# Attention to SSD passage: the time-step chain on 128 partitions, its projections around tile 1's norm, norms by columns, later transposes

## The chip, the cores and the metric

The kernel runs on one core of a Trainium2 chip. The metric is the device time of one execution in microseconds (us). The engines are PE (matmuls), PEld (weight loads), DVE (vector), ACT (scalar functions and copies), POOL (GpSimd) and SP, which issues most of the DMAs. A difference of under 0.3% is not told apart from none here.

## The reference

Two layers over a latent of 1024 tokens and a context of 256, width 1024: gated windowed attention, then a gated bidirectional Mamba-2 SSD mixer. Cut to what the change touches:

```python
# every layer: u = rms_normalize(h) * (1 + scale) + shift; h = h + gate * mixer(u)
def rms_normalize(x):
    return x * lax.rsqrt(jnp.mean(x * x, axis=-1, keepdims=True) + EPS)

def front(h):                       # SSD mixer, for ctx and for the latent
    z, xbc, dt_raw = jnp.split(h @ w_in, [...], axis=-1)
    xbc = jax.nn.silu(centred_depthwise_conv(xbc, conv_w, conv_b))
    xs, bm, cm = jnp.split(xbc, [...], axis=-1)
    dt = jax.nn.softplus(dt_raw.reshape(..., 2, GROUPS, HEADS_PER_GROUP) + dt_bias)
    return z, xs, bm, cm, dt

# scan of one direction, chunks of 128 tokens
da = dt * -exp(a_log)
a_cs = jnp.cumsum(da, axis=2)       # within the chunk
decay_to_end = jnp.exp(a_last - a_cs)
states = einsum(bm, decay_to_end, x * dt)
h_next = exp(a_last) * h_prev + states
y = einsum(cm . bm, exp(a_cs_q - a_cs_s), x * dt) + einsum(cm, h_prev, exp(a_cs))
```

The time steps dt are 64 numbers a token: 32 heads in each of two directions. The backward direction cumulates from the end of a chunk.

## The kernel before

**Tiles.** Tokens are cut into tile 0 and tile 1 (512 latent tokens each) and tile 2 (the 256 context tokens). Activations lie with features on partitions. Every matmul operand is split into a high and a low part (`wh`, `wl` from a raw weight tile `wr`: ACT copy L212 or L952, POOL or DVE difference L214 or L956; `uH`, `uL` of the activations), and a product is three matmuls (L226 to L228, or L1003 and L1012 in the SSD's own loops), each of 256 or 512 columns.

**The end of the attention layer.** `out_steps(i)` yields, for a tile, eight steps `one(m)` and then `fin`. A step loads two halves of an output weight (L219), loads the residual, projects, adds the gated product to the residual on DVE (L723, into `h1k` for tile 1), stores it (L724), squares it on ACT (L727 for m = 0, else L730) and adds the square to the sum `sqa` on POOL (L731). `fin` makes the norm with `rstd`: one matmul with a matrix of ones (L258), a square root on ACT (L260, whose table has to be loaded), a reciprocal on DVE (L261). Then `modulate` runs for each of eight 128-row chunks: DVE multiplication by r (L287), ACT scale and shift (L288), ACT copy to `uH` (L289), DVE difference to `uL` (L290). The steps of tiles 2 and 0 are spread among the attention blocks of tile 1; those of tile 1 come last.

**The other norm.** `rstd_c` and `rstd_n` exist already and serve the first layer's norm. One matmul for each 128 tokens puts the sums on partitions (L342, one column), ACT scales them (L350), POOL raises four numbers a partition to the power -1/2 (L351), DVE spreads them on a diagonal (L353), a matmul with ones broadcasts it (L355), ACT copies the result out (L357).

**The time steps.** `ssd_consts` loads the dt weights (L841, split at L843 and L845), projects tiles 2, 0 and 1 to 64 rows (64 dt numbers on partitions, tokens along the row), evicts with the bias (L862), and runs one chain for the context and tile 0 (64 x 768) and one for tile 1 (64 x 512). A chain is the softplus (L870 to L881, with Exp and Ln on ACT), the logarithm of dt (L882), the two cumulative sums (L886, L887, one for each direction), a store of them to DRAM (L888), the totals and their exponentials (stores L895, L897), differences and exponentials (L900 to L906). Then each 128-token chunk is turned with PE transposes of 64 x 64 (L910, L913, L914, L917 into `psX`; two chunks, the context's, need only the first) and copied out by ACT (L911, L915, L916, L918) and DVE (L919, `vd`). Last, `eal` is read back to all partitions (L920). All ten chunks are turned in `ssd_consts`.

**The SSD's front.** `front(g)` is a generator for one group of heads. It projects, weight column by weight column, bT, two x tiles (x0, x1) and cT, each for the context (`psD`, L1003) and the latent (`pj2`, L1012), followed by the convolution taps and silu as `post` steps, and, for the first three, transposes (L976) that ACT copies out (L979). Then come the gates z (L1037, 256 columns). `post` is a list of steps worked off between matmuls; an entry `(LATE, steps)` waits until so many us of matmuls have gone by. Two groups interleave in slots later: a slot handles a chunk and a direction, with states (L1106, L1164), the POOL product `xw` (L1081), and so on.

**What sets the order.** A scheduler fixes each engine's order when the kernel is built; DMAs of SP run in the order of its queue. In the SSD layer the weight pools `wr`, `wh`, `wl` have two buffers each.

Of the kernel before, what the change touches and what calls it, by code (L numbers as in the profile page):

```python
# [58 lines left out]
LATE = 3.0  # L59
SEGS = (1.5, 2.0, 2.0, 2.2, 2.2)  # L60
# [42 lines left out]
class Kernel:  # L103
# [581 lines left out]
    def attention(self, c0, ckv):  # L685
# [21 lines left out]
        def out_steps(i):  # L707
            s, n = TT[i]
            c = 0 if i < 2 else 1
            st = {}  # L710

            def one(m):
                p = self.po
                w = self.load_halves(a["wo"][m], nc.gpsimd)
                yield
                h1 = t(self.o1, [P, n], F32, "h1k") if i == 1 else t(p, [P, n], F32, "h1")
                if i == 1:
                    st[m] = h1
                nc.sync.dma_start(h1, self.xin(i)[m * P : (m + 1) * P, :])
                out = []  # L720
                yield from self.proj_g(out, ps, w, oH, oL, i, "S" if i == 1 and m % 3 else "pj", parts=1 if i == 1 else PARTS)
                pj = out[0]
                nc.vector.scalar_tensor_tensor(h1, in0=pj[:, :n], scalar=self.mod[0][:, 16 + m, c : c + 1], in1=h1, op0=ALU.mult, op1=ALU.add)  # L723
                nc.sync.dma_start(self.h_d[m][i], h1)  # L724
                if m == 0:
                    st["acc"] = t(p, [P, n], F32, "sqa")
                    nc.scalar.activation(st["acc"], h1, AF.Square)  # L727
                else:
                    sq = t(p, [P, n], F32, "ut")
                    nc.scalar.activation(sq, h1, AF.Square)  # L730
                    nc.gpsimd.tensor_tensor(st["acc"], st["acc"], sq, op=ALU.add)  # L731

            def fin():
                yield
                p = self.po
                r = self.rstd(p, ps, st["acc"], n, D)
                self.alloc_u(i)
                for k in range(KT):
                    if i == 1:
                        h = st[k]  # L740
                    else:
                        h = t(p, [P, n], F32, "h1")
                        nc.sync.dma_start(h, self.h_d[k][i])
                    self.modulate(1, h, r, i, k)

            return [lambda m=m: one(m) for m in range(KT)] + [fin]
# [65 lines left out]
    def ssd_consts(self, p):  # L812
# [25 lines left out]
        eal_d = t(dr, [1, 64, NT], F32, "eald")  # L838
# [3 lines left out]
        wh = t(q, [P, KT, 64], F32R, "wdth")  # L842
        nc.scalar.copy(wh, wr)  # L843
        wl = t(q, [P, KT, 64], F32R, "wdtl")
        nc.vector.tensor_sub(wl, wr, wh)  # L845
        db = t(q, [64, 1], F32, "db")
        nc.sync.dma_start(db, a["dt_bias"])
        al = t(q, [64, 1], F32, "al")
        nc.sync.dma_start(al, a["a_log"])
        nc.scalar.activation(al, al, AF.Exp)  # L850
        nc.vector.tensor_scalar_mul(al, al, -1.0)
        keep = t(q, [64, 6, P], F32, "keep")
        nc.vector.memset(keep, 1.0)
        nc.vector.memset(keep[:32, :, 0:1], 0.0)
        nc.vector.memset(keep[32:, :, P - 1 : P], 0.0)
        keep = keep.rearrange("p c n -> p (c n)")
        dts = t(q, [64, LAT + CTX], F32, "dt")
        where = {0: 0, 2: 512, 1: 768}
        for i in (2, 0, 1):
            n = TT[i][1]  # L860
            pj = self.proj(ps, (wh, wl), i, tag="psX", m=64)
            nc.scalar.activation(dts[:, where[i] : where[i] + n], pj[:64, :n], AF.Identity, bias=db)  # L862
        for lo, n, chunks in ((0, 768, (0, 1, 2, 3, 8, 9)), (768, 512, (4, 5, 6, 7))):
            nb = n // P
            dt = dts[:, lo : lo + n]
            if lo:
                q = self.pool("dtp2", ctx=self.cdt, side="right")
            w1, w2, w3 = [t(q, [64, n], F32, x) for x in ("w1", "w2", "w3")]

            nc.vector.scalar_tensor_tensor(w1, in0=dt, scalar=-1.0, in1=dt, op0=ALU.mult, op1=ALU.min)  # L870
            nc.scalar.activation(w1, w1, AF.Exp)
            nc.vector.tensor_scalar_add(w2, w1, 1.0)
            nc.vector.tensor_scalar_add(w3, w2, -1.0)
            nc.vector.tensor_sub(w1, w1, w3)
            nc.scalar.activation(w2, w2, AF.Ln)
            nc.scalar.activation(w3, w2, AF.Exp, scale=-1.0)
            nc.vector.tensor_mul(w1, w1, w3)
            nc.vector.tensor_add(w1, w1, w2)
            nc.vector.scalar_tensor_tensor(dt, in0=dt, scalar=0.0, in1=w1, op0=ALU.max, op1=ALU.add)
            ln = w2  # L880
            nc.vector.tensor_scalar_max(ln, dt, 1.0e-38)  # L881
            nc.scalar.activation(ln, ln, AF.Ln)  # L882
            da = w1
            nc.vector.tensor_scalar(out=da, in0=dt, scalar1=al, scalar2=None, op0=ALU.mult)
            acs = w3
            nc.vector.tensor_tensor_scan(out=acs[:32], data0=keep[:32, :n], data1=da[:32], initial=0.0, op0=ALU.mult, op1=ALU.add)  # L886
            nc.vector.tensor_tensor_scan(out=acs[32:, ::-1], data0=keep[32:, :n][:, ::-1], data1=da[32:, ::-1], initial=0.0, op0=ALU.mult, op1=ALU.add)  # L887
            nc.sync.dma_start(self.acs_d[:, chunks[0] * P : chunks[0] * P + 512], acs[:, :512])  # L888
            av = acs.rearrange("p (c n) -> p c n", n=P)
            tot = t(q, [64, 6], F32, "tot")[:, :nb]  # L890
            nc.vector.tensor_copy(tot[:32], av[:32, :, P - 1])
            nc.vector.tensor_copy(tot[32:], av[32:, :, 0])
            et = t(q, [64, 6], F32, "et")[:, :nb]
            nc.scalar.activation(et, tot, AF.Exp)
            nc.sync.dma_start(eal_d[0][:, chunks[0] : chunks[0] + 4], et[:, :4])  # L895
            if nb > 4:
                nc.sync.dma_start(eal_d[0][:, 8:10], et[:, 4:])  # L897

            nc.vector.tensor_sub(ln, ln, acs)

            dd = w1
            nc.vector.tensor_sub(dd.rearrange("p (c n) -> p c n", n=P), tot.unsqueeze(2).broadcast_to([64, nb, P]), av)
            nc.scalar.activation(dd, dd, AF.Exp)
            nc.vector.tensor_mul(dd, dd, dt)
            ea = t(q, [64, n], F32, "ea")
            nc.scalar.activation(ea, acs, AF.Exp)  # L906
            for b, c in enumerate(chunks):
                sl = slice(b * P, (b + 1) * P)
                pt = t(ps, [P, 256], F32, "psX")
                nc.tensor.transpose(pt[:, 0:64], dd[:, sl], self.ident[:64, :64])  # L910
                nc.scalar.copy(self.dtdec[:, c, :], pt[:, 0:64])  # L911
                if c < NCH:
                    nc.tensor.transpose(pt[:, 64:128], ea[:, sl], self.ident[:64, :64])  # L913
                    nc.tensor.transpose(pt[:, 128:192], dt[:, sl], self.ident[:64, :64])  # L914
                    nc.scalar.copy(self.eacs[:, c, :], pt[:, 64:128])  # L915
                    nc.scalar.copy(self.dtb[:, c, :], pt[:, 160:192])  # L916
                    nc.tensor.transpose(pt[:, 192:256], ln[:, sl], self.ident[:64, :64])  # L917
                    nc.scalar.copy(self.vf[:, c, :], pt[:, 192:224])  # L918
                    nc.vector.tensor_sub(self.vd[:, c, :], pt[:, 224:256], self.vf[:, c, :])  # L919
        nc.sync.dma_start(self.eal, eal_d.broadcast_to([P, 64, NT]))  # L920
# [18 lines left out]
    def front(self, g, st, post, first=None):  # L939
# [50 lines left out]
        loads = [wx(x) for x, _ in tiles] + [wz(0), wz(1)]  # L990
# [3 lines left out]
        for n, (x, kind) in enumerate(tiles):  # L994
# [3 lines left out]
            wh, wl = cur["h"], cur["l"]  # L998
            if nat:
# [9 lines left out]
            for k in range(KT):  # L1009
                for y, (l, r) in enumerate(((wh, uH), (wh, uL), (wl, uH))):  # L1010
                    for i in range(2):
                        nc.tensor.matmul(raw[:, 512 * i : 512 * i + 512], l[:, k, :], r[i][:, k, :], start=k + y == 0, stop=k == KT - 1 and y == 2)  # L1012
                        yield N512
                if k == 3:
                    post.extend(w["steps"])
# [9 lines left out]
        w0, w = w, loads[5]()  # L1025
# [27 lines left out]
    def ssd(self, c0):  # L1053
# [8 lines left out]
        ps2 = self.pool("scan", ctx=c0)  # L1062
# [447 lines left out]
def layout(i):  # L1510
# [33 lines left out]
    d["w_dt"] = tiles(w[:, SW + 4096 :], 64)[0]  # L1544
# [4 lines left out]
    d["dt_bias"] = np.ascontiguousarray(i["ssd_dt_bias"].reshape(64, 1))  # L1549
    d["a_log"] = np.ascontiguousarray(i["ssd_a_log"].reshape(64, 1))  # L1550
# [19 lines left out]
```

## Time and profile before

| | |
|---|---|
| three runs | 1858.62, 1858.65, 1863.06 us; median 1858.65 |
| the profiled execution | span 1862.4 us, from its first instruction to its last; its time isn't given apart from the span |
| PE busy | 1769.6 us, 95% |
| DVE, ACT, POOL busy | 1183.0, 901.0, 811.6 us |
| tile 1's output stage and its norm | about 718 to 791 us |
| dt chains, front of group 0 | about 773 to 898 us |
| slots of the SSD layer | about 898 to 1770 us |

Rows of the trace name a line of the kernel, an engine, an operation and its tile as out<-in. A time in brackets is idle time of the engine before the instruction, with what ended it. Matmuls are pipelined: their durations overlap, so the pace is read from their starts. The granted clock is a share of the full clock of PE.

### The profile page before, as it was taken

The page shows a single profiled execution, that of the slowest core. Times are in us where ns is not written, and L with a number is a line of the kernel's source. Part 1 is how long each engine was busy: PE and PEld are TensorE (multiplying, and loading weights), DVE is VectorE, ACT ScalarE, POOL GpSimd, SP SyncE. Part 2 cuts the span into 40 slices and gives each one's busy share as a digit, 9 for nine tenths or more (in the row PEclk, how much of TensorE's full clock was granted, in tenths as well). Part 3 has the DMA queues.
Part 4 walks back from the last instruction along what each step waited for, and adds up shares of the span by engine and source line. Part 5 has one row for each costly group of instructions (what it writes and reads, how often), then busy time and mean ns, then how long its engine had stood idle before and what let it go on. Part 6 is the DMA issues. An engine that isn't in the chain of part 4 may idle for free. (4 is left out here: it accounts for less than half of the span.)

```text
span 1862.4 us, 29131 instructions
## 1 busy us (share of the span) xinstructions
PE 1769.6 (95%) x10372; PEld 1511.9 (81%) x10372; DVE 1183.0 (64%) x2137; ACT 901.0 (48%) x1962; POOL 811.6 (44%) x1070
## 2 busy tenths in 40 slices
PE   6899998899999899879999999999999999999997
PEld 2797776788889687668889898888989898888886
DVE  4634426787777756575586767677575767675633
ACT  3812225677778765563353434444353534444422
POOL 2331107654456364401465454545455454554321
PEclk9899999999999999989999999999999999999998
DMA  9557846553444445211232223233223323455542
GB/s 347 197 145 252 256 146 152 127 123 93 95 123 131 111 138 187 97 47 41 60 91 80 79 78 78 71 101 75 77 79 78 78 79 91 148 168 172 179 136 68
DMA packets 212561, 226.84 MB, mean 122 GB/s; under 512 B 16832, under 2 KB 149824, under 8 KB 212416
## 3 DMA queue, kind: packets, MB, share of 16 engines
q1 hardware_dynamic: 178352, 206.33, 36.7%
q0 software_dynamic: 34064, 18.65, 5.5%
q8 instruction: 82, 1.34, 0.3%
q14 instruction: 63, 0.52, 0.1%
HBM read 190.09 MB, written 35.13 MB: 121 GB/s over the span
## 5 line engine op out<-in xcount | busy, mean ns | idle before, releaser
L226 PE MATMUL pj<-uH,wh 128*128 128x512 f32 (+1 forms) x712 | 257.8, 364 | 16.8 <-ACT uH L445 7.2
L227 PE MATMUL pj<-uL,wh 128*128 128x512 f32 (+1 forms) x712 | 245.8, 345 | 0.8 <-DVE uL L446 0.4
L228 PE MATMUL pj<-uH,wl 128*128 128x512 f32 (+1 forms) x712 | 244.6, 344 | 0.0
L1081 POOL TENSOR_TENSOR xw<-xn,dtdec 128x256 f32<-128x256 f32 x144 | 103.6, 722 | 187.2 <-PE psD L1106 113.2
L226 PEld LDWEIGHTS pj<-uH,wh 128*128 128x128 f32 x712 | 136.8, 192 | 46.8 <-issue 10.2
L1012 PE MATMUL pj<-uH,wh 128*128 128x512 f32 x512 | 165.3, 400 | 4.0 <-ACT xn L979 3.8
L1012 PE MATMUL pj<-uL,wh 128*128 128x512 f32 x512 | 166.9, 402 | 0.0
L1012 PE MATMUL pj<-uH,wl 128*128 128x512 f32 x512 | 165.1, 399 | 0.0
L214 POOL TENSOR_TENSOR wl<-wr,wh 128x512 fp32r<-128x512 f32 x92 | 122.4, 1335 | 88.4 <-ACT wh L212 87.7
L665 DVE TENSOR_TENSOR pl<-pt,ph 128x512 fp32r<-128x512 f32 x168 | 114.4, 687 | 64.5 <-ACT ph L664 63.8
L1037 PE MATMUL pj<-wh,uH 128*128 128x256 f32 x512 | 149.4, 292 | 2.5 <-ACT xn L979 2.5
L1037 PE MATMUL pj<-wh,uL 128*128 128x256 f32 x512 | 150.1, 293 | 0.0
L227 PEld LDWEIGHTS pj<-uL,wh 128*128 128x128 f32 x712 | 136.9, 192 | 15.6 <-issue 2.2
L228 PEld LDWEIGHTS pj<-uH,wl 128*128 128x128 f32 x712 | 136.5, 192 | 15.4
L1037 PE MATMUL pj<-wl,uH 128*128 128x256 f32 x512 | 148.4, 290 | 0.0
L212 ACT CAST wh<-wr 128x512 fp32r<-128x512 f32 (+1 forms) x132 | 84.7, 645 | 116.1 <-PE pj L227 84.1
L639 DVE CUSTOM_DVE_ANT_0 sm<-S,mask,nsink 128x640 f32<-128x640 f32 (+2 forms) x160 | 119.4, 772 | 24.3 <-PE S L636 14.5
L664 ACT CAST ph<-pt 128x512 fp32r<-128x512 f32 x168 | 97.3, 585 | 58.7 <-PE pt L660 55.2
L641 ACT ACTIVATE sm<-sm,nm 128x640 f32<-128x640 f32 (+2 forms) x160 | 118.6, 742 | 12.7 <-DVE nm L639 12.3
L1012 PEld LDWEIGHTS pj<-uH,wh 128*128 128x128 f32 x512 | 94.2, 188 | 23.9 <-ACT xn L979 4.8
L1012 PEld LDWEIGHTS pj<-uL,wh 128*128 128x128 f32 x512 | 95.6, 188 | 19.5
L1012 PEld LDWEIGHTS pj<-uH,wl 128*128 128x128 f32 x512 | 95.5, 188 | 19.1
(336 smaller groups left out, 4864.9 us busy)
## 6 DMA issues: line engine op xcount, KB each, us to landing
wr<-w_x SPq DMA_DIRECT2D x32, 512.0 KB, 4.0
M<-acs SPq DMA_DIRECT2D x64, 256.0 KB, 4.9
bw<-acs SPq DMA_DIRECT2D x64, 256.0 KB, 4.9
wr<-wo SPq DMA_DIRECT2D x48, 256.0 KB, 2.7
wr<-w_sk SPq DMA_DIRECT2D x24, 512.0 KB, 4.3
wr<-wg SPq DMA_DIRECT2D x40, 256.0 KB, 3.6
qs<-q POOLq DMA_DIRECT2D x40, 256.0 KB, 3.7
wada<-w_ada SPq DMA_DIRECT2D x16, 512.0 KB, 7.7
```

The lines of the kernel that those rows point to most:

```text
L212: nc.scalar.copy(h, raw)
L214: (eng or nc.vector).tensor_tensor(l, raw, h, op=ALU.subtract)
L226: self.nc.tensor.matmul(ps, lh, rh, start=first and i == 0, stop=False)
L227: self.nc.tensor.matmul(ps, lh, rl, start=False, stop=False)
L228: self.nc.tensor.matmul(ps, ll, rh, start=False, stop=last and i == n - 1)
L639: nc.vector.tensor_tensor_reduce(out=sm[:, :W], in0=Sv, in1=self.mask[:, m0 : m0 + W], scale=-SCALE, scalar=self.nsink[:, 4 * j + r : 4 * ...
L641: nc.scalar.activation(sm[:, :W], sm[:, :W], AF.Exp, bias=nm[:, r : r + 1], scale=-1.0, accum_out=sums[:, r : r + 1])
L664: nc.scalar.copy(ph, ptf)
L665: nc.vector.tensor_sub(pl, ptf, ph)
L1012: nc.tensor.matmul(raw[:, 512 * i : 512 * i + 512], l[:, k, :], r[i][:, k, :], start=k + y == 0, stop=k == KT - 1 and y == 2)
L1037: nc.tensor.matmul(pj[:, c], l, r[:, k, :], start=c % 2 + q + k + y == 0, stop=c % 2 == 1 and q == 1 and k == 3 and y == 2)
L1081: nc.gpsimd.tensor_tensor(xw, X(st, c).rearrange("p (r h) -> p r h", r=R), self.dtdec[:, c, hd(d, g)].unsqueeze(2).broadcast_to([P, R, HP] ...
```

## The change

- The three norms of layer 1 go by columns (`rstd_c`) rather than by `rstd`.
- For tile 1 the squares are added on DVE rather than POOL.
- The dt weights, bias and `a_log` are repeated on the host so that each direction's 32 columns come twice; the projection then fills 128 partitions with the same numbers twice, and of each copy half of the tokens are kept (`dt_raw`, four ACT evictions). A chain works on 128 x 384 (context and tile 0) or 128 x 256 (tile 1) elements.
- The dt projections of tiles 2 and 0 are issued between tile 1's last output step and its `fin`. Tile 1's dt projection becomes an entry of `front(0)` behind bT's, with its own load of the dt weights, and its chain a `post` step (`dt_tail`), with temporaries in the scan pool.
- Chain 0's transposes follow it; chain 1's are `post` entries with delays of 10 and 13. A transpose is 128 x 128 and turns two chunks at once.
- bT's latent projection in `front(0)` runs tile 0 first, then tile 1, rather than both alternately.
- The cumulative sums are stored in 4 DMAs a chain rather than 1, the exponentials in 8 and 4 rather than 2 and 1.

```diff
@@ out_steps
-                    nc.gpsimd.tensor_tensor(st["acc"], st["acc"], sq, op=ALU.add)
+                    (nc.vector if i == 1 else nc.gpsimd).tensor_tensor(st["acc"], st["acc"], sq, op=ALU.add)
...
-                r = self.rstd(p, ps, st["acc"], n, D)
+                r = self.rstd_c(p, st["acc"], n, D, rout=(p, [P, n], F32, "sqa"), dout=(p, [P, 512], F32, "dg0"))
@@ end of attention
-            for f in out_steps(1):
+            steps = out_steps(1)
+            for f in steps[:-1]:
                 for _ in f():
                     pass
+            self.dt_setup()
+            for i, lo in ((2, 256), (0, 0)):
+                n = TT[i][1] // 2
+                self.dt_raw(self.dts[:, lo : lo + n], self.proj(ps, self.wdt, i), n)
+            for _ in steps[-1]():
+                pass
@@ ssd_consts
-        wr = t(self.wp, [P, KT, P], F32, "wr")[:, :, :64]
...
-        for i in (2, 0, 1):
-            n = TT[i][1]
-            pj = self.proj(ps, (wh, wl), i, tag="psX", m=64)
-            nc.scalar.activation(dts[:, where[i] : where[i] + n], pj[:64, :n], AF.Identity, bias=db)
-        for lo, n, chunks in ((0, 768, (0, 1, 2, 3, 8, 9)), (768, 512, (4, 5, 6, 7))):
...
+        self.dt_chain(0, self.dts, self.keep, lambda y, n: t(q, [P, n], F32, y))
+
+    def dt_raw(self, dst, pj, n):
+        for q in range(4):
+            sl = slice(32 * q, 32 * q + 32)
+            self.nc.scalar.activation(dst[sl], pj[sl, q % 2 * n : q % 2 * n + n], AF.Identity, bias=self.dtbias[sl])
+
+    def dt_chain(self, x, dt, keep, tmp):
...
+        for y in range(4):
+            d, s = y // 2, 512 * x + 256 * (y % 2)
+            nc.sync.dma_start(self.acs_d[32 * d : 32 * d + 32, s : s + 256], acs[32 * y : 32 * y + 32, :256])
...
+            for k, src in enumerate(srcs):
+                nc.tensor.transpose(pt[:, k].rearrange("p d h r -> p (d h r)"), src[:, sl], self.ident)
...
+        if x:
+            return [lambda b=b: block(b) for b in range(nb)]
+        for b in (2, 0, 1):
+            block(b)
+
+    def dt_tail(self, raw, post):
...
+        self.dt_raw(dt, raw, 256)
+        steps = self.dt_chain(1, dt, self.dt_keep(t(pc, [P, 256], F32, "hf")), lambda y, n: t(pc, [P, n], F32, tags[y]))
+        self.nc.sync.dma_start(self.eal, self.eal_d.broadcast_to([P, 64, NCH + NCC]))
+        post.extend([(d, [f]) for d, f in zip(DTLATE, steps)])
@@ front
+        if g == 0:
+            tiles.insert(1, (None, "dt"))
+        loads = [(lambda: weights(a["w_dt"], KT, P)) if x is None else wx(x) for x, _ in tiles] + [wz(0), wz(1)]
...
+            if x is None:
+                raw = t(ps, [P, 512], F32, "psX")
+                for k in range(KT):
+                    for y, (l, r) in enumerate(((wh, uH), (wh, uL), (wl, uH))):
+                        nc.tensor.matmul(raw, l[:, k, :], r[1][:, k, :], start=k + y == 0, stop=k == KT - 1 and y == 2)
+                        yield N512
+                    if k == 3:
+                        post.extend(w["steps"])
+                post.append(lambda raw=raw: self.dt_tail(raw, post))
+                continue
...
-            for k in range(KT):
-                for y, (l, r) in enumerate(((wh, uH), (wh, uL), (wl, uH))):
-                    for i in range(2):
-                        nc.tensor.matmul(raw[:, 512 * i : 512 * i + 512], l[:, k, :], r[i][:, k, :], start=k + y == 0, stop=k == KT - 1 and y == 2)
+            for q in ((0,), (1,)) if g == 0 and n == 0 else ((0, 1),):
+                for k in range(KT):
+                    for y, (l, r) in enumerate(((wh, uH), (wh, uL), (wl, uH))):
+                        for i in q:
+                            nc.tensor.matmul(raw[:, 512 * i : 512 * i + 512], l[:, k, :], r[i][:, k, :], start=k + y == 0, stop=k == KT - 1 and y == 2)
@@ host
+    twice = np.concatenate([np.arange(32 * x, 32 * x + 32) for x in (0, 0, 1, 1)])
+    d["w_dt"] = tiles(w[:, SW + 4096 :][:, twice])[0]
```

In the order that the scheduler gives, tile 1's dt projection stands behind x0's on PE, between chain 0's transposes and x1.

More of the change, by code (lines that the diff above doesn't have):

```diff
@@ L863, in ssd_consts @@
-        for lo, n, chunks in ((0, 768, (0, 1, 2, 3, 8, 9)), (768, 512, (4, 5, 6, 7))):
[L864 to L911, printed above, removed]
-                if c < NCH:
[L913 to L919, printed above, removed]
@@ L920, in ssd_consts @@
-        nc.sync.dma_start(self.eal, eal_d.broadcast_to([P, 64, NT]))
+        self.wdt = wh, wl
+        self.dtbias = t(self.cp, [P, 1], F32, "db")
+        nc.sync.dma_start(self.dtbias, a["dt_bias"])
+        self.aneg = t(self.cp, [P, 1], F32, "al")
+        nc.sync.dma_start(self.aneg, a["a_log"])
+        nc.scalar.activation(self.aneg, self.aneg, AF.Exp)
+        nc.vector.tensor_scalar_mul(self.aneg, self.aneg, -1.0)
+        self.keep = self.dt_keep(t(q, [P, 384], F32, "keep"))
+        self.dts = t(q, [P, 384], F32, "dt")
@@ L989, in front @@
         st["sz"] = []
-        loads = [wx(x) for x, _ in tiles] + [wz(0), wz(1)]
+        if g == 0:
+            tiles.insert(1, (None, "dt"))
+        loads = [(lambda: weights(a["w_dt"], KT, P)) if x is None else wx(x) for x, _ in tiles] + [wz(0), wz(1)]
         w = first or loads[0]()
@@ L1024, in front @@
         need(w)
-        w0, w = w, loads[5]()
+        w0, w = w, loads[-1]()
         post.extend(w["steps"])
```

100 lines of the change are left out of this document (78 added, 22 removed).

## The prediction

> **What bounds the kernel now.** I read the page first, for the busy shares.
>
> ```profile
> span 1862.4 us, 29131 instructions
> PE 1769.6 (95%) x10372; PEld 1511.9 (81%) x10372; DVE 1183.0 (64%) x2137; ACT 901.0 (48%) x1962; POOL 811.6 (44%) x1070
> ```
>
> PE is the bound: all its idle time is 1862.4 - 1769.6 = 92.8 us, so the change can win only by removing PE idle time, by taking PE out of a low clock, or by giving it less work. So the second view is PE's waits in the passage that the change rewrites, 765 to 900 us (line waited at, releaser, us in total, times, longest).
>
> ```profile
> PE psX L913 <- ACT dtdec L911: 5.2, 3, 4.2
> PE pj L258 <- POOL sqa L731: 3.4, 1, 3.4
> PE psX L917 <- ACT dtb L916: 1.9, 4, 1.1
> PE pj L976 <- ACT xn L979: 1.6, 1, 1.6
> PE pj L1012 <- ACT xn L979: 1.5, 1, 1.5
> ```
>
> These five are 13.6 us, and two of the names are those of the dt transposes. A low clock adds to them. The windows (length, busy time and count of each engine, then granted clock, DMA share, GB/s) show it:
>
> ```profile
> 745.00:750.00 5.00, 2.46 (x8) 1.70 (x9) 3.13 (x4) 4.26 (x7) 3.48 (x2) 0.91 0.78 248
> 750.00:755.00 5.00, 5.00 (x18) 4.00 (x17) 3.73 (x4) 1.33 (x3) 2.43 (x2) 0.75 0.80 278
> ...
> 810.00:820.00 10.00, 5.53 (x27) 3.91 (x26) 8.50 (x14) 5.81 (x13) 0.00 (x0) 0.87 0.23 67
> 820.00:830.00 10.00, 6.40 (x31) 4.61 (x31) 7.73 (x16) 6.86 (x35) 0.00 (x0) 0.50 0.09 33
> 830.00:840.00 10.00, 8.48 (x42) 7.71 (x42) 5.64 (x5) 4.14 (x9) 1.04 (x1) 0.78 0.37 105
> ```
>
> From 820 to 830 PE runs at half clock, and at 0.78 in the ten us behind. The third view, PE in order of time, gives the boundaries (start, duration, idle before in brackets):
>
> ```profile
> 768.83 0.39 PE L228 MATMUL S<-uH,wl 128*128 128x512 f32 x1
> 772.64 1.74 PE L258 MATMUL pj<-sqa,ones 128*128 128x512 f32 x2 [3.42 <-POOL sqa L731]
> ...
> 776.09 0.41 PE L226 MATMUL psX<-uH,wdth 128*64 128x256 f32 x1
> 776.30 0.34 PE L227 MATMUL psX<-uL,wdth 128*64 128x256 f32 x1
> ...
> 777.86 0.28 PE L228 MATMUL psX<-uH,wdtl 128*64 128x256 f32 x1
> 777.97 0.39 PE L226 MATMUL psX<-uH,wdth 128*64 128x512 f32 x1
> ...
> 783.23 0.39 PE L228 MATMUL psX<-uH,wdtl 128*64 128x512 f32 x1
> 783.45 0.28 PE L1003 MATMUL psD<-uH,wh 128*128 128x256 f32 x1
> ...
> 814.39 0.63 PE L1012 MATMUL pj<-uH,wl 128*128 128x512 f32 x2
> 819.18 0.37 PE L913 MATMUL psX<-ident,ea 64*128 64x64 f32 x1 [4.16 <-ACT dtdec L911]
> ...
> 829.03 1.11 PE L976 MATMUL pj<-ident,cacc 128*128 128x128 f32 x4
> ...
> 866.65 0.45 PE L1037 MATMUL pj<-wh,uH 128*128 128x256 f32 x1
> ```
>
> Starts, not durations, give the pace: 24 matmuls of 512 columns start between 777.97 and 783.23, 0.229 us apart; two of 256 columns are 0.11 apart at full clock (777.86, 777.97) and 0.21 just behind the long wait (776.09, 776.30). So a dt projection of tile 0 or 1 (24 matmuls) is 5.5 us, of tile 2 (the context) 2.8; a weight column of `front` is 2.8 + 11 = 13.8. Doubling the dt columns from 64 to 128 doesn't change the 512 that stream past them: it costs PE nothing. The last projection matmul ahead of the dt transposes (two of 0.23 from 814.39) is over at 814.85; the transposes of the first x tile follow at 829.03. In these 14.2 us PE has 34 dt transposes. I take 0.11 for each, as for 256 columns (these have 64, so it is an upper value): 3.7 us. The other 10.5 are waits and low clock. This stage is what the change is worth.
>
> **The change, part by part. 1, the passage to tile 1's norm.** Before, the out-projection ends at 768.83 + 0.23 = 769.06 and PE stands until the sum of squares is through:
>
> ```profile
> 765.88 6.70 POOL L731 TENSOR_TENSOR sqa<-sqa,ut 128x512 f32<-128x512 f32 x5
> 770.77 1.28 ACT L260 ACT_TABLE_LOAD   x1
> 775.13 3.35 DVE L261 RECIPROCAL sqa<-sqa 128x512 f32<-128x512 f32 x1 [5.12 <-ACT sqa L260]
> 778.52 4.90 DVE L287 TENSOR_TENSOR h1k<-h1k,sqa 128x512 f32<-128x512 f32 x8
> ```
>
> Five sums of 1.3 us queue on POOL until 772.58. The last square ends where the table load begins, 770.77; a DVE pass of this size is 4.90/8, some 0.65 us, so on DVE the sum would be ready at 771.45. It no longer matters: PE now has the context's dt projection for that time (769.06 + 2.8 = 771.85). Then comes the norm by columns, which the trace has in the first norm:
>
> ```profile
> L342 PE MATMUL pt<-ones,sqa 128*128 128x1 f32 x8 | 1.9, 355 | 0.0
> L355 PE MATMUL pt<-sqt,ones 128*128 128x512 f32 x2 | 1.1, 644 | 0.0
> ```
>
> The column matmuls take 1.9 (to 773.75); tile 0's dt projection, issued next, covers the ACT, POOL and DVE steps and ends at 779.25; the broadcast matmuls cost 1.1, to 780.4. ACT must first evict tile 0's dt in four pieces, then copies the broadcast: r is ready at about 781.7, against 778.5 before (start of L287). So **r is not earlier, but 3.2 us later**, though the table load and the 3.35 us reciprocal are gone. Behind r everything modulated is late: the L290 that ends a chunk.
>
> ```profile
> L290 DVE TENSOR_TENSOR uL<-h1k,uH x8: 676/682/693, 783.3 to 790.7; 128x512 fp32r<-128x512 f32 x8
> ```
>
> Its last one starts 12.2 us after the first multiplication, so now at about 793.9. PE has the context (2.8) and the tile 0 half of bT (5.5) meanwhile, 780.4 to 788.7; that is why bT is split by halves. The tile 1 half needs the chunks as they come, stands idle about 2.0 and ends at 796.3; the context transposes wait about 0.95. At 797.5 PE has done what before had done at 803.0 less tile 1's dt projection, 5.5: also 797.5. **Gain here: 0.** (Before lost 3.4 to the sum and some 1.9 to low clock; after pays 1.9 for column matmuls and 3 in waits.) If PE found the tile 1 half unready for longer, each us would count in full; if r came 3 us earlier (the broadcast not held behind the dt projection and its evictions), the 3 of waits would be gone. Bounds: -3 to +3.
>
> **2, chain and transposes.** Chain 0 (context and tile 0) now works on 128 x 384 elements rather than 64 x 768, so every DVE and ACT pass is half as long in columns; the table loads stay. It begins at 781, as tile 1's dt needn't be waited for, and I place its end at 809, while PE reaches its nine transposes at 812.2: no wait. x0's low weights can only be split when a buffer that bT's weights held is free: a wait of about 0.9. Chain 1 is the second chain before, from tile 1's eviction to the end of the last product:
>
> ```profile
> 797.84 0.67 ACT L862 ACTIVATE dt<-psX,db 64x512 f32<-64x512 f32 x1
> 819.90 0.68 DVE L904 TENSOR_TENSOR w<-w,dt 64x512 f32<-64x512 f32 x1 [1.27 <-ACT w L903]
> ```
>
> That is 22.7 us. The new one has half the columns and no first chain beside it, but still its table loads; I take 16. Its projection follows x0 (about 819), so it is done at 836.1; PE has x1 in between and reaches the eight transposes at 835.3: a wait of 0.9. Sum of this stage against before: +10.5 (waits in the 14.2 us); +2.2 for the ten us at clock 0.78 that follow; +1.8 for 17 transposes of 128 columns at no more than 0.11 instead of 34 (3.7 - 1.9); +1.5, the wait at L1012, which stands right behind the stage while ACT has 34 small copies; -0.9 - 0.9. **Gain 14.2.** The z projection should start at 866.65 - 14.2 = 852.5. The SP queue gets 8 acs stores for 2 and 12 eald stores for 3; the eal, M and bw loads wait behind them. Issue of such a store holds the queue for half a us:
>
> ```profile
> 806.46 0.49 SPq L888 DMA_DIRECT2D acs<-w  x1
> ```
>
> 15 more stores are 7 us; eal is needed only by the state chain behind x1, so cT's 11 us cover them, and without that cover up to 7 would be lost.
>
> **3, upstream.** The norms of tiles 2 and 0 also go by columns, +1.9 us of PE for tile 0, half (0.9) for tile 2. What they can win is what PE waits for there, and the output stage before 769 is short of weights:
>
> ```profile
> PE pj L226 <- ACT sqa L260: 0.8, 1, 0.8
> PE pj L226 <- ACT uH L682: 0.8, 1, 0.8
> PE S L226 <- ACT wh L212: 2.6, 1, 2.6
> ```
>
> The first is tile 2's, the second tile 0's (with 0.3 more at L227 behind it). 2.8 - 0.8 - 1.1 = 0.9 lost. The dt weights come doubled, 0.25 MB more; at the 248 GB/s of 745 to 750, where PE stands 2.5 of 5 us, that is 1.0 us, all of it on the path because L212 waits for the same queue. One wo load moves ahead of eight residual loads on SP, which I can't price from the trace: -1 to +4. **Loss 1.9.** The al and bias loads go to the start of the kernel, where PE waits for other loads anyway: 0, at most 2.
>
> Net: 14.2 - 1.9 = 12.3. The profiled execution's span of 1862.4 stands 3.75 above the median, 1858.65; the same gap for after gives a span near 1850.1 and a **time of 1846.3 us**. Bounds: the parts at their best (-3, -1, no 0.9 waits) 1840; at their worst (+3, +4, +2) 1855.
>
> The low clock is where a rule could weigh against the sum. After's two waits near 796 (2.0 and 0.95) are short; in the trace the clock was down to 0.75 at 750 to 755 behind waits of 2.6 and 1.1 at L226 and L228, so by that row they cost another 1.3 us (a quarter of 5). The Trainium skill, "TensorE: Matmul & The Clock Gate", Part 1 (The HAM clock gate), says that the clock is halved after an idle window of about 3.4 us; by that, gaps of 2 us cost nothing more. The 3.42 and 4.16 us waits agree with it, the row at 750 less so. I take none and keep 1.3 in the range.
>
> **The rivals.** *Chain 1 late.* It has as many instructions and table loads as before, and now shares DVE and ACT with x0's and x1's taps. If it takes 22.7 again, it ends at 842.8; PE, whose transposes have a fixed place, waits 7.5 in place of 0.9, over the length of the 4.16 that was followed by a half clock, +2.5: 1846.3 + 6.6 + 2.5 = 1855.4. For: passes on 256 columns keep the fixed part. Against: the two chains of before were interleaved, each waiting for the other.
>
> *Hidden afterwards.* The gain is made ahead of z, and what comes behind (loads of w_z, M and bw on SP behind 15 more stores, the state chain) may start no earlier. If z starts at 862 in place of 852.5, 9.5 go: 1855.8.
>
> *The change doesn't do what it says.* If transposes issued later still meet an unfinished chain in both groups, the 10.5 stay and 1.9 is lost: about 1859.
>
> *Slower.* The slots behind 898 us, 64 steps of one direction and chunk, are PE-bound to within a per cent:
>
> ```profile
> PE psX L1164 <- POOL xw L1081: 4.6, 5, 1.0
> ...
> 898.00:1007.00 109.00, 108.62 (x673) 97.48 (x672) 74.13 (x126) 45.77 (x103) 58.17 (x79) 1.00 0.30 82
> 1007.00:1116.00 109.00, 106.08 (x667) 94.90 (x666) 74.40 (x126) 45.93 (x106) 57.03 (x77) 1.00 0.28 78
> ```
>
> Where POOL's product comes late, a slot pays 4.6/5 = 0.92. Entering the slots with two transposes and post steps displaced could lock the late order into all 64: 59 - 4.6 = 54 lost, about 1900. It outweighs the 12.3 from 12.3/64 = 0.19 a slot on, and is slower by the bound from 0.28. For: five slots do pay it. Against: PE's order in the slots, as built, settles within one slot into the cycle that before reaches too.
>
> **How the numbers follow.** Forecast 0.68, range of its own 1840 to 1854; chain 1 late 0.08, hidden 0.08, doesn't do what it says 0.04, slots 0.12. A difference within 0.3% (5.6 us: 1853.1 to 1864.2) can't be told from none. Faster: nearly all of the forecast (0.67) and a third of the next two (0.05): 0.72. Slower: 0.12, the slots. Same: the rest, 0.16. The range runs from 1838 (all bounds at their best and the rest of the 3.4 us at L976/L1012 gone) to 1861, over the two hidden cases and the one without effect.
>
> **What would show it.** Right: no wait of 3 us ahead of the norm's first matmul; the first multiplication of tile 1 about 12.6 us after the out-projection's end (9.5 before); no wait above 1 us at the dt transposes and clock 1.00 around them; z about 83 us after the out-projection (97.6 before); the 12.3 whole at the first slot and still there at the end. Wrong: a wait of over 3 us at the second group of transposes (chain 1 late); a z start that has not moved; xw waits in most slots; an output stage longer by over 4 us.

## The result, and the profile after

The changed kernel took 1850.4 us (median of 4 runs, 1847.9 to 1852.1), the kernel before 1860.3 in its four (the three shown and one more). The ratio is 0.9943, 95% interval 0.993 to 0.9957: 0.57% faster, some 10.6 us by the ratio (the two medians differ by 9.9). A second set of runs gave 0.9944 (0.9926 to 0.9962); in it one run of the kernel before took 2845.34 us and is left out as a slow one.

The page of the changed kernel:

```profile
span 1850.4 us, 29176 instructions
PE 1764.7 (95%) x10375; PEld 1506.2 (81%) x10375; DVE 1171.9 (63%) x2144; ACT 894.8 (48%) x1963; POOL 803.8 (43%) x1066
```

PE's idle time fell from 92.8 to 1850.4 - 1764.7 = 85.7 us, PE's busy time by 4.9 (busy time is longer at half clock, so a clock that stays up shows here). PE's waits from 760 to 892 us of the changed kernel (its lines are shifted: L943 are the dt transposes, L1022 the transposes of `front`, L1061 and L1071 its context and latent projections, L1096 the gates z, L882 the dt evictions, L1025 the copies of transposed tiles):

```profile
PE pj L1071 <- ACT bn L1025: 2.4, 1, 2.4
PE pj L1022 <- ACT xn L1025: 1.4, 1, 1.4
PE pj L1071 <- DVE uL L291: 1.1, 3, 0.6
PE psD L1022 <- DVE cctx L983: 1.0, 1, 1.0
PE pj L227 <- ACT dt L882: 0.8, 1, 0.8
PE pj L1071 <- DVE wl L1002: 0.7, 1, 0.7
```

The 5.2 + 1.9 us at the dt transposes and the 3.4 us ahead of the norm are gone; no row of L943 is left. A new wait stands first: 2.4 us, where x1's latent projection needs a PSUM buffer out of which ACT has not yet copied `bn`. PE in order of time, the landmarks only:

```profile
766.48 0.39 PE L229 MATMUL S<-uH,wl 128*128 128x512 f32 x1
769.53 0.95 PE L343 MATMUL pt<-ones,sqa 128*128 128x1 f32 x8
771.25 0.51 PE L227 MATMUL pj<-uH,wdth 128*128 128x512 f32 x1 [0.78 <-ACT dt L882]
...
795.35 0.44 PE L1022 MATMUL psD<-ident,cctx 128*128 128x128 f32 x2 [0.98 <-DVE cctx L983]
...
810.57 0.38 PE L943 MATMUL psX<-ident,w 128*128 128x128 f32 x2
824.22 0.72 PE L1071 MATMUL pj<-uH,wh 128*128 128x512 f32 x2 [2.44 <-ACT bn L1025]
825.96 1.05 PE L1071 MATMUL pj<-uH,wh 128*128 128x512 f32 x2
826.81 1.05 PE L1071 MATMUL pj<-uL,wh 128*128 128x512 f32 x2
827.66 1.05 PE L1071 MATMUL pj<-uH,wl 128*128 128x512 f32 x2
838.03 0.27 PE L943 MATMUL psX<-ident,uT 128*128 128x128 f32 x1
854.49 0.39 PE L1096 MATMUL pj<-wh,uH 128*128 128x256 f32 x1 [0.24 <-ACT xn L1025]
```

From the out-projection's end (766.48 + 0.23 = 766.71) z starts 87.8 us later; before it was 97.6. Behind the new wait pairs of matmuls start 0.85 apart (825.96, 826.81, 827.66) where 0.46 is usual: half clock, as the windows of the changed kernel say (of ten us each; the clock is the third column from the end).

```profile
810.00:820.00 10.00, 9.64 (x58) 8.21 (x57) 7.70 (x14) 6.02 (x23) 1.04 (x1) 1.00 0.60 152
820.00:830.00 10.00, 7.56 (x33) 6.19 (x33) 6.65 (x15) 9.73 (x15) 0.00 (x0) 0.83 0.25 75
830.00:840.00 10.00, 10.00 (x54) 8.36 (x53) 4.69 (x12) 6.38 (x13) 1.60 (x3) 1.00 0.15 47
```

A mean of 0.83 over ten us is a loss of up to 1.7; before had 0.87, 0.50 and 0.78 in these three windows, 8.5 in all by the same measure. The gain is kept to the end: the first slot's matmul starts at 880.6 (892.8 before), and of the slots' waits the first is little changed (6.7 us in 7 against 4.6 in 5):

```profile
PE psX L1223 <- POOL xw L1140: 6.7, 7, 1.0
```

### The profile page after: what moved, and what is told of

It is laid out like the page before. It is cut to its first block, busy times and chain, and to the rows that moved or that the text cites. A ratio compares the mean times of both kernels' runs of the same rounds, so it can differ in the third digit from the quotient of the medians.

```text
span 1850.4 us, 29176 instructions
## 1 busy us (share of the span) xinstructions
PE 1764.7 (95%) x10375; PEld 1506.2 (81%) x10375; DVE 1171.9 (63%) x2144; ACT 894.8 (48%) x1963; POOL 803.8 (43%) x1066
## 5 line engine op out<-in xcount | busy, mean ns | idle before, releaser
L1071 PE MATMUL pj<-uH,wh 128*128 128x512 f32 x512 | 165.6, 399 | 4.4 <-ACT bn L1025 2.4
L1071 PE MATMUL pj<-uL,wh 128*128 128x512 f32 x512 | 167.8, 401 | 1.1 <-DVE uL L291 1.1
L1071 PE MATMUL pj<-uH,wl 128*128 128x512 f32 x512 | 167.2, 401 | 0.7 <-DVE wl L1002 0.7
L215 POOL TENSOR_TENSOR wl<-wr,wh 128x512 fp32r<-128x512 f32 x92 | 123.0, 1341 | 88.3 <-ACT wh L213 87.8
L1096 PE MATMUL pj<-wh,uH 128*128 128x256 f32 x512 | 151.0, 295 | 2.6 <-ACT xn L1025 2.6
L1096 PE MATMUL pj<-wh,uL 128*128 128x256 f32 x512 | 149.1, 291 | 0.0
L1096 PE MATMUL pj<-wl,uH 128*128 128x256 f32 x512 | 146.4, 286 | 0.0
L665 ACT CAST ph<-pt 128x512 fp32r<-128x512 f32 x168 | 97.4, 585 | 58.9 <-PE pt L661 55.3
L1071 PEld LDWEIGHTS pj<-uH,wh 128*128 128x128 f32 x512 | 94.7, 189 | 25.0 <-ACT bn L1025 2.6
L1071 PEld LDWEIGHTS pj<-uL,wh 128*128 128x128 f32 x512 | 96.6, 189 | 21.9 <-DVE uL L291 2.0
L1071 PEld LDWEIGHTS pj<-uH,wl 128*128 128x128 f32 x512 | 96.4, 189 | 20.5 <-DVE wl L1002 1.1
```

Of the source, the lines that this page charges most:

```text
L215: (eng or nc.vector).tensor_tensor(l, raw, h, op=ALU.subtract)
L665: nc.scalar.copy(ph, ptf)
L1096: nc.tensor.matmul(pj[:, c], l, r[:, k, :], start=c % 2 + q + k + y == 0, stop=c % 2 == 1 and q == 1 and k == 3 and y == 2)
```

## The experiments

The passage is measured below as the start of the first z matmul less the start of DVE's last gated residual (L723 or L724; 769.26 in the kernel before, 766.90 in the changed one): two rows of the same execution, so it is free of what happened earlier. Each entry is one profiled execution. r is the start of the first multiplication by the norm, and "transposes" the start of the first transpose of each of the two groups, both counted from that residual. The ratios' intervals reach 0.0009 to 0.002 to either side.

| kernel | ratio to before | r after | transposes after | passage us |
|---|---|---|---|---|
| before, twice | 1 | 9.3, 9.8 | | 97.4, 97.0 |
| changed, twice | 0.9943, 0.9944 | 12.7, 12.6 | 43.7, 71.1 and 43.8, 70.4 | 87.6, 86.8 |
| tiles 2 and 0 with the old norm | 0.9954 | 12.7 | 44.7, 70.3 | 86.7 |
| tile 1 with the old norm | 0.9999 | 18.9 | 43.8, 76.9 | 97.3 |
| tile 0's dt behind the broadcast | 1.0008 | 8.3 | 34.1, 64.1 | 99.6 |
| bT not by halves | 1.0011 | 12.7 | 42.3, 76.0 | 99.2 |
| sum on POOL | 1.0001 | 17.2 | 35.4, 64.2 | 99.0 |
| before with the norms by columns | 1.0007 | 8.3 | | 95.0 |
| tile 1's dt evicted by DVE | 0.9928 | 12.7 | 44.0, 68.0 | 85.6 |
| the same, and bn's second copy, twice | 0.9930, 0.9956 | 12.7, 12.6 | 43.7, 68.8 and 45.2, 69.2 | 86.4, 86.7 |
| all dt evictions on DVE | 0.9957 | 12.2 | 44.5, 68.8 | 86.4 |

**1. The two kernels again.** No edit.

> The changed kernel, profiled a second time. Between the first two profiles the clock of PE fell in some places with the same waits in both (350 to 360 us: 0.83 before, 1.00 after) or with waits that differ by tenths. Theory A: those falls outside the passage are luck of the execution, so the second profile has some of them elsewhere, and the gain of 2.4 us up to the end of the output projection moves by 1 to 3 us. Theory B: it is the change's, and stays within 0.5. Inside the passage both expect the wait of 2.4 us at x1's latent projection (released by ACT's copy of bn) and the low clock behind it to be there again. Time ratio 0.993 to 0.996.

> The kernel before, profiled a second time, for the same question from the other side. Theory A: the falls to 0.83 at 350, 620, 750 and 775 us do not all come back. Theory B: they do. Both: the waits of 3.4 us (sum of squares) and 4.2 us (dt transposes), and the half clock behind the second, come back.

The wait came back (3.1 us), and with it the passage, within 0.8 us. The clock did not repeat. In the passage of the second profile it stayed up behind the long wait and fell from 790 to 800 instead:

```profile
825.62 0.73 PE L1071 MATMUL pj<-uH,wh 128*128 128x512 f32 x2 [3.11 <-ACT bn L1025]
790.00:800.00 10.00, 8.29 (x26) 5.30 (x26) 7.53 (x14) 9.15 (x13) 0.00 (x0) 0.83 0.08 14
820.00:830.00 10.00, 6.89 (x40) 5.96 (x40) 6.58 (x15) 9.75 (x18) 0.00 (x0) 1.00 0.28 81
```

From 350 to 360 us, in the attention layer, where neither the code nor PE's busy time differ, the windows of before, of the changed kernel and of the changed kernel again are:

```profile
350.00:360.00 10.00, 7.31 (x37) 5.92 (x36) 6.76 (x14) 5.95 (x15) 5.90 (x9) 0.83 0.57 132
```

```profile
350.00:360.00 10.00, 7.31 (x45) 5.98 (x44) 7.24 (x16) 6.68 (x16) 5.89 (x9) 1.00 0.62 144
```

```profile
350.00:360.00 10.00, 7.32 (x26) 5.56 (x25) 6.05 (x11) 4.89 (x13) 5.07 (x9) 0.66 0.63 132
```

There the clock is luck of an execution, worth 0 to 3.4 us of these ten (Theory A); from 620 to 630 too, where the kernel before has 0.83 and then 1.00. The other two places named ahead are not shown to be luck: from 750 to 755 the kernel before has 0.75 and 0.91, from 775 to 780 it has 0.86 and 0.68, and the changed kernel 1.00 in all four cases. At the last residual the changed kernel was 2.4 us ahead in the first pair of profiles and 1.9 in the second (767.5 against 769.4). At the first of the 24 residuals 0.8 and 2.3 of that were there already (535.9 and 537.8 before, 535.0 and 535.5 after): between first and last lie 233.4 and 231.5 us before, 231.9 and 232.0 after. The output stage is about as long as it was: over the nine other profiles below whose norms of tiles 2 and 0 go by columns it is 230.7 to 232.9.

**2. Tiles 2 and 0 with the old norm.**

```diff
-r = self.rstd_c(p, st["acc"], n, D, ...)
+r = self.rstd_c(p, st["acc"], n, D, ...) if i == 1 else self.rstd(p, ps, st["acc"], n, D)
```

> Tiles 2 and 0 get the old norm (ones matmul, square root, reciprocal) again; the rest stays as changed. The prediction had the norm by columns cost 0.9 us more PE than it saves there, so it expects this version 0.9 us faster than the changed kernel (end of the output projection 0.9 us earlier). The rival, from the two profiles: it saves about 2 us there (the wait at L226 behind the square root, the delayed attention blocks behind the 3.35 us reciprocal), so this version is 1 to 2.5 us slower and the waits on the square root and a reciprocal of 1.75 and 3.35 us are back.

The ratio, 0.9954 (0.9937 to 0.997), can't be told from the changed kernel's. The trace has the wait at tile 2's norm back:

```profile
PE pj L227 <- ACT sqa L261: 0.8, 1, 0.8
```

From the first to the last residual it takes 232.8 us, against 231.9 and 232.0: the rival's sign, a gain of about 1 rather than a loss of 0.9, but of a size that two executions of the kernel before differ by.

**3. Tile 1's dt evicted by DVE.** What stood ahead of `bn` on ACT in the changed kernel:

```profile
818.49 1.28 ACT L1203 ACTIVATE M<-M,vf 128x128 f32<-128x128 f32 x4 [3.67 <-DVE M L1197]
819.67 1.03 ACT L998 CAST wh<-wr 128x1024 fp32r<-128x1024 f32 x1
820.61 1.89 ACT L882 ACTIVATE hf<-psX,db 32x256 f32<-32x256 f32 x4
822.52 1.03 ACT L982 ACTIVATE pj<-cacc 128x1024 f32<-128x1024 f32 x1
823.58 0.58 ACT L1025 COPY bn<-pj 128x512 f32<-128x512 f32 x1
```

```diff
-            self.nc.scalar.activation(dst[sl], pj[sl, ...], AF.Identity, bias=self.dtbias[sl])
+            self.nc.vector.tensor_scalar(out=dst[sl], in0=pj[sl, ...], scalar1=self.dtbias[sl], scalar2=None, op0=ALU.add)
```

The edit holds for tile 1's call alone.

> Tile 1's dt is evicted by DVE instead of ACT; nothing else. In the changed kernel ACT does the expansion of M, a weight cast, four dt evictions (1.9 us) and a tanh before the copy of bn that frees the PSUM of x1's latent projection: PE waits 2.44 us and runs at half clock for some 3.4 us behind it (about 1.7 us lost). Theory: 1.9 us of this queue go, the wait falls to 0.6 or less and the clock stays up: 3 to 4 us faster than the changed kernel, z 3 to 4 us earlier. Rival: the wait moves on, to chain 1's transposes, which then meet an unfinished chain (it ended 3.3 us ahead of them), or to the weights' low part on DVE: gain under 1 us.

Of its waits in the passage:

```profile
PE pj L1074 <- ACT xn L1028: 0.8, 1, 0.8
...
PE psX L946 <- DVE uT L933: 0.3, 1, 0.3
...
PE pj L1074 <- ACT bn L1028: 0.2, 1, 0.2
```

The wait on `bn` fell from 2.4 to 0.2 and no window from 800 to 860 us was below full clock: second transposes at 68.0 after the residual, not 71.1 and 70.4. But 1.2 us came back behind them (0.8 on x0's copy, on ACT), and the passage is 85.6, 1 to 2 us shorter, not 3 to 4. The wait was as named; its price in the end was half or less of what I gave it.

**4. Tile 1 with the old norm.** The condition of experiment 2 turned round (`if i != 1`).

> Tile 1 gets the old norm again; the norms of tiles 2 and 0 stay by columns. The scheduler then puts the ones matmul behind both dt projections, some 8 us after the output projection, and square root, table load and reciprocal follow with PE idle less 2.8 + 5.5 us of projections. Theory (the norm by columns is worth something because its small steps hide under tile 0's dt projection): r comes at about 14.5 us after the last output step instead of 12.9, z 1 to 3 us later. Rival, as the prediction had it (the norm by columns gains nothing here, r is set by what PE and ACT do first): z within 1 us.

It lost all that the change had gained: ratio 0.9999 (0.9985 to 1.0013). The ones matmul has to wait for a PSUM buffer that the evictions of tile 0's dt hold, and the square root and reciprocal follow in series. PE, then DVE in that kernel:

```profile
779.09 1.19 PE L259 MATMUL pj<-sqa,ones 128*128 128x512 f32 x2 [1.99 <-ACT dt L882]
```

```profile
782.22 3.35 DVE L262 RECIPROCAL sqa<-sqa 128x512 f32<-128x512 f32 x1 [1.24 <-ACT sqa L261]
```

r came 18.9 us after the residual, not 14.5; the context transposes 33.1 rather than 28.5, and the x0 projection behind them fell into the slow clock (0.83 from 800 to 810). z was some 10 us later, where 1 to 3 was expected.

**5. Tile 0's dt projection behind the broadcast.**

```diff
             for i, lo in ((2, 256), (0, 0)):
                 n = TT[i][1] // 2
-                self.dt_raw(self.dts[:, lo : lo + n], self.proj(ps, self.wdt, i), n)
-            for _ in steps[-1]():
-                pass
+                if i == 2:
+                    self.dt_raw(self.dts[:, lo : lo + n], self.proj(ps, self.wdt, i), n)
+                    for _ in steps[-1]():
+                        pass
+                else:
+                    with self.tc.issue_after(self.bcast.ins):
+                        self.dt_raw(self.dts[:, lo : lo + n], self.proj(ps, self.wdt, i), n)
```

`self.bcast` is the broadcast matmul (L355 before).

> Tile 0's dt projection is held until the norm's broadcast matmul has been issued; the change issues it ahead. r should come at about 9.5 us after the last output step instead of 12.9. Theory of the prediction (its bound of -3): the chunk-bound part of bT, three waits of 3 us together, goes, but PE stands some 4 us ahead of the broadcast and may fall to half clock (1.7 us), chain 0 starts some 5 us later, so z comes between 1 us earlier and 2 us later. Rival: the order in which the change does it costs 3 us, and z is 2 to 3 us earlier.

r came at 8.3, 4.4 us earlier than in the changed kernel, and z 12 later, where at most 2 was expected: the ratio is 1.0008 (0.9995 to 1.0021). Its waits in the passage:

```profile
PE psX L947 <- DVE uT L934: 4.0, 1, 4.0
PE psD L1026 <- DVE cctx L987: 3.8, 2, 2.3
PE pt L356 <- DVE dg L354: 3.0, 1, 3.0
PE psX L947 <- DVE w L934: 2.8, 1, 2.8
```

The 3.0 at the broadcast is the cover taken away. The others are later: chain 0, whose input now comes later, and chain 1 are both unfinished when PE reaches their transposes (2.8 and 4.0), because the scheduler also set both groups earlier in PE's order (34 and 64 us after the residual instead of 44 and 71).

**6. bT not by halves.**

```diff
-            for q in ((0,), (1,)) if g == 0 and n == 0 else ((0, 1),):
+            for q in ((0, 1),):
```

> bT's latent projection alternates between tile 0 and tile 1 again. Theory: PE meets the first unready chunk of tile 1 at once instead of after 5.5 us of tile 0's half; the scheduler fills with other work, but the chunk-bound waits grow from about 1.6 to 4 us and more, and z is 2 to 5 us later. Rival: since PE ends with the last chunk either way (at about 27 us after the output projection), splitting is worth under 1 us.

Ratio 1.0011 (0.9999 to 1.0023). The largest waits:

```profile
PE pj L1071 <- ACT wh L998: 4.4, 1, 4.4
PE psD L1022 <- DVE cctx L983: 2.6, 1, 2.6
PE pj L1071 <- DVE uL L291: 2.3, 1, 2.3
PE pj L1071 <- ACT xn L1025: 1.9, 1, 1.9
PE pj L1071 <- ACT bn L1025: 1.6, 1, 1.6
PE pj L1071 <- ACT uH L290: 1.4, 1, 1.4
```

The chunk waits grew as expected (2.3 + 1.4); the 4.4 behind them, x0's weights that ACT splits later, I had not foreseen. PE's waits in the passage come to 16.6 us, against 8.5 in the first profile of the changed kernel, and five windows of ten us stand at 0.83 to 0.95, against one at 0.83: about the 12 us by which z is later.

**7. The sum on POOL, and the norms by columns alone in the kernel before.** The first takes DVE out of the sum again; the second puts `rstd_c` and the DVE sum into the old kernel, and leaves the dt work alone.

> Tile 1's squares are added on POOL again, the rest as changed. The prediction: it no longer matters by more than the 0.8 us that the sum is late behind the context's dt projection; z within 1 us. Rival, from the other undone parts, each of which lost all that the change had gained: the order that the scheduler makes then is another one, and z is 5 us or more later.

> The kernel before, with only the three norms by columns and tile 1's sum on DVE; dt as before. The prediction's terms alone (upstream 2.8 us more PE, 1.9 less waits; at tile 1 the sum 1.2 us earlier and r some 1 to 2 us earlier than with the reciprocal, with PE idle for most of it) give -1 to +2 us against before. Rival: the norm by columns is a gain of its own of 3 us or more, as undoing it at tile 1 in the changed kernel cost 10.

The sum on POOL costs as much as the other undone parts: ratio 1.0001 (0.9987 to 1.0016). The last addition of that kernel and, below it, of the changed one:

```profile
769.63 1.26 POOL L732 TENSOR_TENSOR sqa<-sqa,ut 128x512 f32<-128x512 f32 x1 [0.50 <-ACT ut L731]
768.41 0.69 DVE L732 TENSOR_TENSOR sqa<-sqa,ut 128x512 f32<-128x512 f32 x1 [0.76 <-ACT ut L731]
```

They end 2.9 and 2.2 us after the last residual (768.02 and 766.90): the sum is 0.7 us later. Its norm on PE:

```profile
778.11 0.95 PE L343 MATMUL pt<-ones,sqa 128*128 128x1 f32 x8
782.47 2.08 PE L356 MATMUL pt<-dg,ones 128*128 128x512 f32 x2 [3.41 <-DVE dg L354]
```

The built order is another one: tile 0's dt projection stands ahead of the column matmuls, which start at 778.11 instead of 769.53, and nothing is left to cover the small steps behind them (3.41 idle). Two thirds of the context's dt projection also stand among the matmuls of the last output step, so the 99.0 us of this passage leave out some 2 us of work that the others have in it. The norms by columns alone gave 1.0007 (0.9998 to 1.0016), no gain in time, though the passage of its one profile is 2 us shorter: the prediction's terms, not the rival.

**8. More evictions on DVE.** The first version moves the second copy of `bn` (`nc.vector.tensor_copy`) as well; the second moves the dt evictions of tiles 2 and 0 instead.

> As the version with tile 1's dt evicted by DVE, and the second copy of bn moves to DVE too. There the wait at x1's projection had fallen from 2.4 to 0.2 us but 1.2 us came back behind the second transposes (cT's projection waits for x0's copy on ACT). Theory: one ACT copy less ahead of x0's copies gives some of this back; z 0.3 to 1 us earlier than with the first version, 2.5 to 3 us earlier than in the changed kernel. Rival: DVE, with chain 1's passes queued there, is as full as ACT: no difference or up to 1 us later than the first version.

> All dt evictions go to DVE: tile 1's, as in the first such version, and those of tile 2 and tile 0 around tile 1's norm. ACT's four evictions of tile 0 (1.9 us) no longer stand ahead of the copy of the broadcast. Theory: tile 0's projection no longer waits 0.8 us for the eviction of tile 2's (DVE is free there), r comes about 1.5 to 2 us earlier, the chunk-bound waits of bT (1.6 us) shrink below 0.8, and z is 2 to 3 us earlier than with tile 1's eviction alone, so about 83.5 us after the last output step. Rival: bT's end is set by the eight chunks on ACT and DVE, which now also has the evictions; z within 0.7 us of that version.

> The version with tile 1's dt and the second copy of bn on DVE once more, since its first interval (0.991 to 0.995) overlaps that of the changed kernel (0.993 to 0.996). If its 2 to 3 us inside the passage are real, the median stands 12 to 15 us below before's again (ratio 0.992 to 0.9935) and z comes 86 us or less after the last output step (changed kernel 86.8 and 87.6). Rival, that the first result was a lucky start of the kernel (its profile was 3 us ahead at the first attention block already): ratio 0.994 or more.

Passages of 86.4, 86.7 and 86.4 us: none shorter than with tile 1's eviction alone (85.6). With the copy moved, PE waits 1.0 us for it on DVE instead. With all evictions on DVE, ACT's copy of the broadcast no longer waits behind them, but DVE's multiplications wait for DVE's evictions:

```profile
780.45 1.97 DVE L883 TENSOR_SCALAR dt<-pj,db 32x256 f32<-32x256 f32 x4 [4.48 <-PE pj L229]
782.45 4.90 DVE L288 TENSOR_TENSOR h1k<-h1k,sqa 128x512 f32<-128x512 f32 x8
```

The 1.9 us changed engines; r gained 0.5, and a wait of 2.1 us at x0's weights came in. The two results of the version with two moves, 0.9930 and 0.9956, differ by more than its gain, so none of these is shown to beat the changed kernel.

Delays of 0 instead of 10 and 13 for chain 1's transposes were not run: the built order is the same on every engine, so the delays don't set their place. What does is not shown.

## Why the prediction came out

**Direction, mechanism and total: right.** -12.3 was forecast, -10.6 measured. The time was 1850.4 where 1846.3 was forecast, inside the range; 1.6 of these 4.1 us are the kernel before, 1860.3 in this set and 1858.65 in the first. The waits at the sum and at the dt transposes went, r came 12.9 us after the out-projection's end (12.6 forecast, 9.5 before), the context transposes at 28.6 (28.4), and the first group of dt transposes at 43.9 (43.1) without a wait. The slots kept the gain, so that rival is out; POOL's late product was waited for 7 times, not 64. Of the signs named, z about 83 us after the out-projection (87.8) and a clock of 1.00 around the transposes (0.83 from 820 to 830) did not hold.

The main term, the 10.5 us at the dt transposes, rests on the traces: the waits there are gone, and they come back where the transposes are set earlier (2.8 and 4.0 us in experiment 5, where they end 34 and 64 us after the residual; 1.7 and 3.7 with the sum on POOL). At the later places, 44 and 71, these chains would have been done. No run has the chains on 64 partitions with the later place; how much the 128 partitions add is not shown.

**The stage: mis-sized, 14.2 forecast, about 10 measured** (97.2 to 87.2, means of two). The step that was off is the one from the first transposes to the second, put at 24.0 us (812.2 to 836.2, its wait of 0.9 included); it measured 27.4 and 26.6. Of the 3 us, 2.4 to 3.1 are the wait on `bn`, a step that was missing: I took what DVE and ACT do behind bT as hidden, and did not ask what tile 1's four dt evictions (1.89 us, where one of 64x512 took 0.67) push back on ACT. The rest is the half clock behind it (1.7, in one of the two profiles) and bT's transposes among these matmuls (about 1), which I left out. In return the 0.9 at chain 1's transposes did not come: the chain takes 14.2 us (820.61 to 834.8, the end of its last product), 16 was assumed, so "chain 1 late" is out too. These parts come to 0.7 to 0.9 us more than the step lost; the forecast doesn't split its 24.0, so that remainder stays open.

**Upstream: a loss of 1.9 forecast, none found.** Column matmuls are there, but the stage is as long as before within 1 to 2 us, the spread between executions. The 2.8 of PE was mis-sized: I took the price from the first norm's row (1.9 for eight column matmuls), but in the changed kernel tile 2's four take 0.50 us (607.61) and tile 0's eight 1.00 (721.29 and 721.97), as tile 1's take 0.95. That leaves a loss of 0.6 by the same sum. Whether the 1.0 for the 0.25 MB of weights was paid is not shown. Two errors of opposite sign, 4 and 2 us, made the sum look better than its terms: that much of its closeness is luck.

**Span and median.** Times stand 1.7 us above the span of the same execution (1852.09 and 1850.4), so the profile of before was an execution of 1864.1, not one that lies 3.75 over its time. Its clock at 350 and 620 us was low without the change having a part in it.

**"It no longer matters" and "r gains nothing": right against before, wrong as prices.** Compared with before, the passage up to the context transposes gained nothing, as forecast, and the norm by columns alone gained nothing (experiment 7). But I took r 3 us earlier as worth up to 3, and the order that brought it 4.4 earlier cost 12; I took the sum's engine as worth 0.8, and it was worth 11. In the changed order each of these parts hides another: tile 0's dt projection hides the column norm's small steps, the early dt starts chain 0 soon enough, the halves give PE work while chunks come. Undo one and the schedule, with it the whole gain, is lost. What was shown is this loss; how much of it is the missing cover and how much the order that the scheduler makes instead was not separated.

## What to carry to other kernels

Parts of a change that cover each other can't be priced one by one: alone in the old kernel the norm was worth nothing, and undoing any one of four parts of the new one cost all 10 us. Where a change gives an engine more pieces of work, list what queues behind them there, evictions above all: a PSUM buffer that is copied out 2.4 us late is the next wait. And where a scheduler fixes the order at build time, compare the built orders first: with a sum 0.7 us late two groups of matmuls stood the other way round, and a delay that reads like a control changed nothing.

## What was not expected of the hardware

The clock fell to half behind waits well under 3 us, and not each time: 1.7 us lost behind a wait of 2.44 us, none behind one of 3.1 us in the same place of the same kernel's second profile; 0.83, 1.00 and 0.66 at 350 to 360 us with PE busy 7.31, 7.31 and 7.32 of ten. In the second profile of the changed kernel it fell even behind four waits of 0.2 to 0.6 us that end between 789.25 and 792.75: matmuls of 512 columns then start 0.43 apart (793.11, 793.54, 793.97). In the first profile the same four waits are followed by matmuls 0.23 apart. The Trainium skill, "TensorE: Matmul & The Clock Gate", Part 1 (The HAM clock gate), gives an idle window of about 3.4 us that runs freely. That the outcome varies agrees with a free-running window, but falls behind shorter waits differ from it, and here the measurement decides: a few of PE's short waits can cost 1.7 us more, or nothing, in one execution or the next.
